# Gate and up projections as 2x2 block products with seven products for eight, and a down projection in four parts

## The chip, the cores and the metric

The kernel runs on one core of a Trainium2 chip. The metric is the device time of one execution in microseconds (us); lower is better. The engines are named as in the profile: PE is TensorE's matrix multiply and PEld its load of the stationary operand, DVE is VectorE, ACT is ScalarE, POOL is GpSimd, SP is SyncE, which here only issues transfers.

## The reference, cut to what matters

A decoder trunk of two layers works on 256 tokens of width 2048. A layer has a mixing part and then a SwiGLU feed-forward network (FFN), and the change lies in the latter:

```
h = rms_norm(x, norm_ffn_w)                            # (256, 2048)
x = x + (silu(h @ w_gate) * (h @ w_up)) @ w_down       # gate, up: 2048 x 5632; down: 5632 x 2048
```

All is float32.

## The kernel before, in words

**Split products.** A float32 number is split into a high half and a low half (a matmul type, fp32r, that PE takes at speed): `xh` and `xl` for activations, `wh` and `wl` for weights. Each product is three matmuls, high x high, low x high, high x low (L343, L344, L345), accumulated in PSUM. The activations are the stationary operand (128 tokens), and a weight tile of 512 columns moves through.

**Weight stream.** All weights of the program are one list of tiles (`plan`, L250), each of a pair of k-tiles: 128 partitions x 2 x 512 columns, 512 KB. `wtile` (L300) is called when PE needs the next tile. It issues loads ahead (`fetch`, L275, on SP's queue, into five `raw` buffers) and prepares the tile after the one in use (`split`, L284): ACT copies `raw` to `wh`, which rounds (L295), and DVE computes `wl = raw - wh` (L296). There are three buffers each of `wh` and `wl`. An engine carries out its instructions in program order; between engines they wait on semaphores for data and for buffers.

**FFN.** `ffn` (L204) goes through the 5632 hidden columns in 11 blocks of 512. For each block `dense` (L319) makes the gate: 8 tiles (pairs of k-tiles), each with 2 k-tiles x 2 token tiles x 3 matmuls. ACT applies silu out of PSUM, scaled by the row's reciprocal norm. A second `dense` makes up, and DVE multiplies the two (L216). The result is transposed by PE (L131) and split into halves `hh`, `hl`, which stay in two of the 22 general buffers (`U`) until the down projection. `FFN_PARTS = [8, 3]`: after 8 blocks, and again after 3, four groups of 512 output columns of the down projection are made from the blocks at hand and added to the residual in SBUF (`add_res`, L183). PSUM has four `dn` tiles for `dense` and four `mx` tiles for the rest.

**Output projection.** Ahead of the FFN, `out_proj` (L188) makes four groups of columns; after each, `post_x` (L354) transposes the new residual, scales it by the norm's weight and splits it into `xh` and `xl`, which the FFN uses.

GpSimd has next to no work in the FFN; it does some small operations of the mixing part (L104) there and in the norms.

Of the kernel before, what the change touches and what calls it, by code (L numbers as in the profile page):

```python
# [21 lines left out]
RWKV_EPS = 64e-5  # L22
EXP_HALF = math.exp(-0.5)

FFN_PARTS = [8, 3]

# [29 lines left out]
class Trunk:  # L56
# [121 lines left out]
    def setup(self):  # L178
        nc, A = self.nc, self.A
        self.plan()  # L180
        self.pp = [self.cp.tile([P, NPP], F32, tag=f"pp{l}", name=f"pp{l}") for l in range(DEPTH)]
# [66 lines left out]
    RAW, SPLIT = 5, 3  # L248

    def plan(self):  # L250
        seq = []
        for l in range(DEPTH):
            off = 0
            for n in (IN_W[name] for name in IN_ORDER):
                seq += [(f"win{l}", off + kp * 2 * P * n, n) for kp in range(8)]
                off += D * n
            for g in range(4):
                seq += [("wout", (l * 4 + g) * D * 512 + kp * 2 * P * 512, 512) for kp in range(8)]
            f0 = 0
            for nf in FFN_PARTS:  # L260
                for f in range(f0, f0 + nf):
                    for w in ("wgate", "wup"):
                        seq += [(w, (l * 11 + f) * D * 512 + kp * 2 * P * 512, 512) for kp in range(8)]
                for g in range(4):
                    seq += [("wdown", (l * 4 + g) * D_FF * 512 + kp * 2 * P * 512, 512)
                            for kp in range(2 * f0, 2 * (f0 + nf))]
                f0 += nf
        self.seq, self.loaded, self.cast, self.used = seq, [], [], 0

    @staticmethod  # L270
    def cuts(i, n):
# [11 lines left out]

    def split(self, upto):  # L284
        nc = self.nc
        while len(self.cast) < min(upto, len(self.seq)):
            i = len(self.cast)
            raw = self.loaded[i]
            if i < len(self.seq) - 2 * FFN_PARTS[-1]:
                wh = self.wp.tile([P, 1024], F32R, tag="wh", name=self.nm("wh"), bufs=self.SPLIT)  # L290
                wl = self.wp.tile([P, 1024], F32R, tag="wl", name=self.nm("wl"), bufs=self.SPLIT)
            else:
                wh, wl = self.U(F32R), self.U(F32R)
            for c in self.cuts(i, self.seq[i][2]):
                nc.scalar.activation(wh[:, c], raw[:, c], AF.Copy)  # L295
                nc.vector.tensor_tensor(wl[:, c], raw[:, c], wh[:, c].bitcast(F32), op=ALU.subtract)  # L296
            self.cast.append((wh, wl))
            self.loaded[i] = None

    def wtile(self, n):  # L300
        i = self.used
        assert self.seq[i][2] == n
        self.fetch(i + self.RAW)
        self.split(i + self.SPLIT - 1)
        self.fetch(i + self.RAW + self.SPLIT - 2)
        r = self.cast[i]
        self.cast[i] = None
        self.used += 1
        return r

# [8 lines left out]
    def dense(self, n, kps, xs, cm):  # L319
# [3 lines left out]
        ps = [self.dps(), self.dps()]  # L323
        last = len(kps) - 1
        for i, kp in enumerate(kps):
            wh, wl = self.wtile(n)
            for j in range(2):
                xh, xl = xs(2 * kp + j)
                st = i == 0 and j == 0
# [8 lines left out]
                else:  # L338
                    c = slice(j * n, (j + 1) * n)
                    for t in range(2):  # L340
# [3 lines left out]
                        nc.tensor.matmul(o, lhsT=xl[:, x], rhs=wh[:, c], start=False, stop=False)  # L344
                        nc.tensor.matmul(o, lhsT=xh[:, x], rhs=wl[:, c], start=False, stop=sp)  # L345
                self.pump()
        return ps


    def new_x(self):  # L350
        self.ssq = self.S(8)
        self.xt = []

    def post_x(self, l, g, wname):  # L354
# [3 lines left out]
        self.transpose_split(lambda t, k: self.res[g][:, t, k * P:(k + 1) * P], xh, xl,  # L358
                             lambda k: self.par(l, wname, g * 4 + k))
        self.xt.append((xh, xl))  # L360
        self.squares(g)

    def squares(self, g):
        sq = self.U()
# [823 lines left out]
    def out_proj(self, l):  # L1188
# [12 lines left out]
        self.finish_x()  # L1201
        self.yt = None

    def ffn(self, l):
        f0 = 0
        xt, rstd = self.xt, self.rstd
        for pi, nf in enumerate(FFN_PARTS):
            hts = []
            for f in range(f0, f0 + nf):
                kps = list(range(8))  # L1210
                ps = self.dense(512, kps, self.xs, False)
                sg = self.evac_tm(ps, 512, AF.Silu)
                ps = self.dense(512, kps, self.xs, False)
                for t in range(2):
                    o = sg[:, t * 512:(t + 1) * 512]
                    self.stt(o, ps[t], rstd[:, t:t + 1], o, ALU.mult, ALU.mult)
                hh = self.v4(self.U(F32R))
                hl = self.v4(self.U(F32R))
                self.transpose_split(lambda t, k: sg[:, t * 512 + k * P:t * 512 + (k + 1) * P], hh, hl, None)
                hts.append((hh, hl))  # L1220
            lastp = pi == len(FFN_PARTS) - 1

            def xs(k):
# [30 lines left out]
    def final(self, kps, xs, fw):  # L1254
# [8 lines left out]
        for t in range(2):  # L1263
            ps = self.dps()
            for i, kp in enumerate(kps):
                if t == 0:
                    ws.append(self.wtile(512))
                wh, wl = ws[i]
                for j in range(2):
                    xh, xl = xs(2 * kp + j)  # L1270
                    c, x = slice(j * 512, j * 512 + 512), slice(t * P, (t + 1) * P)
                    nc.tensor.matmul(ps, lhsT=xh[:, x], rhs=wh[:, c], start=i == 0 and j == 0, stop=False)  # L1272
                    nc.tensor.matmul(ps, lhsT=xl[:, x], rhs=wh[:, c], start=False, stop=False)  # L1273
                    nc.tensor.matmul(ps, lhsT=xh[:, x], rhs=wl[:, c], start=False, stop=i == len(kps) - 1 and j == 1)  # L1274
# [74 lines left out]
    return np.ascontiguousarray(w.reshape(k, 2, P, n).transpose(0, 2, 1, 3)).reshape(-1)  # L1349


def _layout(i):
    i = {k: np.asarray(v) for k, v in i.items()}
    o = {"cst": _constants(), "rm": _ret_mask()}
# [51 lines left out]
    wo, gate, up, down = [], [], [], []  # L1406
    for l in range(DEPTH):
        w = i["w_out"][l]
        part = {0: w[1536:], 1: w[512:1024], 2: w[1024:1536], 3: w[:512]}
        w = np.concatenate([part[n] for n in OUT_ORDER], axis=0)  # L1410
        wo += [_tiles(w[:, g * 512:(g + 1) * 512], 512) for g in range(4)]
        gate += [_tiles(i["ffn_w_gate"][l][:, g * 512:(g + 1) * 512], 512) for g in range(11)]
        up += [_tiles(i["ffn_w_up"][l][:, g * 512:(g + 1) * 512], 512) for g in range(11)]
        down += [_tiles(i["ffn_w_down"][l][:, g * 512:(g + 1) * 512], 512) for g in range(4)]
    o["wout"], o["wgate"], o["wup"], o["wdown"] = (np.concatenate(x) for x in (wo, gate, up, down))
    return o


# [20 lines left out]
```

## Time and profile before

| | |
|---|---|
| time, median of 3 runs (lowest, highest) | 2444.47 us (2444.41, 2446.57) |
| the profiled execution | 2444.33 us, of which the span from first to last instruction is 2442.3 us |
| granted TensorE clock, mean | 0.996 |
| HBM read | 430.66 MB, 178 GB/s over the span |

The profile is taken from one execution. Its page has: 1, the busy time of each engine; 2, the span in 40 slices; 3, the transfer queues; 4, the chain of work that ended last; 5, the costliest groups of instructions (line, engine, operation, output<-inputs, shape, count, busy us, mean ns, idle time ahead of them and what ended it); 6, the transfers. Further views list instructions in order of time (start in us, duration in us, engine, line, operation, and in brackets the idle time of the engine ahead of it with what ended it), and busy times by stretches of the span. `mx` and `dn` are PSUM tiles; `u`, `s`, `wh`, `wl`, `raw`, `xh`, `xl`, `res`, `cc`, `pp` and `vf` lie in SBUF. Matmuls overlap in the pipeline, so the distance of two starts, and not a duration, is what one costs.

### The profile page before, as it was taken

What the parts mean: (1) busy time and instruction counts of PE and PEld (TensorE: products, weight loads), DVE (VectorE), ACT (ScalarE), POOL (GpSimd) and SP (SyncE); (2) the same over time, 40 slices, a digit from 0 to 9 for tenths busy, and PEclk for the clock granted to TensorE, in tenths of its full rate; (3) what the DMA queues carried; (4) which work ended last, traced back from release to release, by engine and by line L of the source; (5) the groups of instructions that cost most, each with busy time, mean ns of one, the idle gap of its engine ahead of it and who ended that gap; (6) DMA issues with size and microseconds to landing.
All of it is one profiled execution on the core that took longest, in us unless ns stands there. A gap on an engine that the chain in (4) does not pass through costs nothing. (4 is left out here: it accounts for less than half of the span.)

```text
span 2442.3 us, 33197 instructions
## 1 busy us (share of the span) xinstructions
PE 2411.7 (99%) x13208; PEld 2050.3 (84%) x13208; DVE 1403.6 (57%) x1722; ACT 1113.1 (46%) x1376; POOL 138.4 (6%) x141
## 2 busy tenths in 40 slices
PE   8999999999999999999999999999999999999998
PEld 8998788888888888888899988888888888888886
DVE  7777656544544544445567876665445454444455
ACT  6445544444444433344454545444444444334444
POOL 3100230000000000000001022200000000000000
PEclk9999999999999999999999999999999999999999
DMA  8454445555555555655544544455555555556554
GB/s 292 147 168 113 146 159 164 186 186 190 188 190 191 188 190 189 207 191 188 181 147 156 166 116 141 156 173 180 190 192 187 191 190 188 190 190 207 192 186 147
DMA packets 139419, 435.97 MB, mean 179 GB/s; under 512 B 30464, under 2 KB 30720, under 8 KB 139264
## 3 DMA queue, kind: packets, MB, share of 16 engines
q1 hardware_dynamic: 137360, 428.52, 53.8%
q0 software_dynamic: 1184, 4.19, 0.5%
q8 instruction: 103, 1.69, 0.3%
q10 hardware_dynamic: 720, 1.15, 0.1%
q14 instruction: 52, 0.43, 0.0%
HBM read 430.66 MB, written 3.15 MB: 178 GB/s over the span
## 5 line engine op out<-in xcount | busy, mean ns | idle before, releaser
L296 DVE TENSOR_TENSOR wl<-raw,wh 128x1024 fp32r<-128x1024 f32 (+3 forms) x811 | 986.8, 1218 | 934.5 <-ACT wh L295 931.1
L295 ACT ACTIVATE wh<-raw 128x1024 fp32r<-128x1024 f32 (+3 forms) x811 | 844.7, 1042 | 1174.8 <-PE dn L344 998.2
L345 PE MATMUL dn<-wl,xh 128*128 128x512 f32 (+2 forms) x1856 | 713.9, 385 | 12.2 <-DVE wl L296 12.2
L343 PE MATMUL dn<-wh,xh 128*128 128x512 f32 (+2 forms) x1856 | 719.7, 388 | 0.0
L344 PE MATMUL dn<-wh,xl 128*128 128x512 f32 (+2 forms) x1856 | 714.2, 385 | 0.0
L345 PEld LDWEIGHTS dn<-wl,xh 128*128 128x128 f32 x1856 | 349.8, 189 | 78.6 <-DVE wl L296 13.6
L343 PEld LDWEIGHTS dn<-wh,xh 128*128 128x128 f32 x1856 | 349.9, 189 | 66.8 <-issue 1.4
L344 PEld LDWEIGHTS dn<-wh,xl 128*128 128x128 f32 x1856 | 349.9, 189 | 65.9 <-issue 1.4
L344 PE MATMUL dn<-wh,u 128*128 128x512 f32 x936 | 369.6, 395 | 0.0
L345 PE MATMUL dn<-wl,u 128*128 128x512 f32 x936 | 368.6, 394 | 0.0
L343 PE MATMUL dn<-wh,u 128*128 128x512 f32 x936 | 368.5, 394 | 0.0
L335 PE MATMUL dn<-xh,wh 128*128 128x256 f32 x896 | 258.5, 289 | 7.2 <-ACT wh L295 7.2
L337 PE MATMUL dn<-xh,wl 128*128 128x256 f32 x896 | 254.6, 286 | 1.1 <-DVE wl L296 1.1
L336 PE MATMUL dn<-xl,wh 128*128 128x256 f32 x896 | 254.9, 285 | 0.0
L343 PEld LDWEIGHTS dn<-wh,u 128*128 128x128 f32 x936 | 175.9, 188 | 39.8
L345 PEld LDWEIGHTS dn<-wl,u 128*128 128x128 f32 x936 | 176.3, 188 | 39.1
L344 PEld LDWEIGHTS dn<-wh,u 128*128 128x128 f32 x936 | 175.9, 188 | 39.6
L335 PEld LDWEIGHTS dn<-xh,wh 128*128 128x128 f32 x896 | 173.4, 194 | 10.0 <-ACT wh L295 7.7
L337 PEld LDWEIGHTS dn<-xh,wl 128*128 128x128 f32 x896 | 172.9, 194 | 1.8 <-DVE wl L296 1.5
L336 PEld LDWEIGHTS dn<-xl,wh 128*128 128x128 f32 x896 | 173.6, 194 | 0.3
L119 ACT ACTIVATE u<-mx 128x512 fp32r<-128x512 f32 (+4 forms) x158 | 73.5, 497 | 65.8 <-PE mx L127 30.2
L101 DVE TENSOR_TENSOR u<-u,u 128x1024 f32<-128x1024 f32 (+26 forms) x175 | 84.4, 487 | 22.5 <-POOL u L104 11.8
(142 smaller groups left out, 1157.6 us busy)
## 6 DMA issues: line engine op xcount, KB each, us to landing
raw<-wgate SPq DMA_DIRECT2D x176, 512.0 KB, 3.4
raw<-wup SPq DMA_DIRECT2D x176, 512.0 KB, 3.4
raw<-wdown SPq DMA_DIRECT2D x176, 512.0 KB, 3.5
raw<-win SPq DMA_DIRECT2D x175, 512.0 KB, 3.6
raw<-wout SPq DMA_DIRECT2D x64, 512.0 KB, 3.4
raw<-win SPq DMA_DIRECT2D x32, 340.0 KB, 2.9
raw<-win SPq DMA_DIRECT2D x16, 360.0 KB, 3.0
u<-xt SPq DMA_DIRECT2D x8, 256.0 KB, 7.7
```

The source lines that it names most:

```text
L101: self.nc.vector.tensor_tensor(out, a, b, op=op)
L119: self.nc.scalar.activation(out, in_, func, **kw)
L295: nc.scalar.activation(wh[:, c], raw[:, c], AF.Copy)
L296: nc.vector.tensor_tensor(wl[:, c], raw[:, c], wh[:, c].bitcast(F32), op=ALU.subtract)
L335: nc.tensor.matmul(o, lhsT=wh[:, c], rhs=xh, start=st and m % 2 == 0, stop=False)
L336: nc.tensor.matmul(o, lhsT=wh[:, c], rhs=xl, start=False, stop=False)
L337: nc.tensor.matmul(o, lhsT=wl[:, c], rhs=xh, start=False, stop=sp and m % 2 == 1)
L343: nc.tensor.matmul(o, lhsT=xh[:, x], rhs=wh[:, c], start=st, stop=False)
L344: nc.tensor.matmul(o, lhsT=xl[:, x], rhs=wh[:, c], start=False, stop=False)
L345: nc.tensor.matmul(o, lhsT=xh[:, x], rhs=wl[:, c], start=False, stop=sp)
```

## The change

The gate and up weights of a block are interleaved on the host: a load now brings one k-tile, with its 512 gate columns and its 512 up columns (`wgu`). For a pair of k-tiles, the two token tiles times two k-tiles of the activations are a 2x2 matrix of blocks A, and k-tiles times (gate, up) are a 2x2 matrix of blocks W. In pairs 1 to 6 (`SEVEN`) the product of the two is made in Winograd's form, from 7 block products in place of 8. In pairs 0 and 7 it is made plainly. All eight results accumulate over pairs: four PSUM tiles C for what goes straight to an output, four PSUM tiles M for what has to be combined.

- Weight side, in `split`: for a Strassen pair, three parts s0, s1, s2. For s0, GpSimd makes three sums of weight blocks into `u1` and `u2` (one operation of 1024 columns, with one operand repeated, and two of 512); the loaded blocks A11/A22 are split by ACT and DVE as before, and the half tile `b` with the remaining block as well. For s1 and s2, `u1` and `u2` are split by ACT and DVE. Parts of the plain pairs (kind "c") have their subtraction on GpSimd. All other tiles (kind "n") are split as before.
- Activation side, in `post_pair`: for each of pairs 1 to 6, four differences and sums of activation blocks (128 columns each) on GpSimd, then halves of them on ACT and DVE, once per layer.
- `gate_up` takes the place of two `dense` calls, and evacuates C and M with eight DVE operations on 512 columns that read PSUM, two that do not, and four on ACT. The transposes of the result are put off (`late`) until the next block's first pair, or the down projection's first tile, has been issued.
- `FFN_PARTS = [3, 3, 3, 2]`: the down projection is made in four parts.

```
-FFN_PARTS = [8, 3]
+FFN_PARTS = [3, 3, 3, 2]
+SEVEN = range(1, 7)
...
+            elif kind == "c":
+                self.cast.append(halve(raw, [slice(0, 1024)], nc.gpsimd))
+            elif kind == "s0":
+                r1 = self.loaded[i + 1]
+                u1, u2 = self.U(), self.U()
...
+                nc.gpsimd.tensor_tensor(v(u1), v(raw), h(r1, 1).rearrange("p (o c) -> p o c", o=1).to_broadcast([P, 2, 512]),
+                                        op=ALU.add)
+                nc.gpsimd.tensor_tensor(h(u2, 0), h(u1, 0), h(raw, 1), op=ALU.add)
+                nc.gpsimd.tensor_tensor(h(u2, 1), h(u2, 0), h(r1, 0), op=ALU.add)
+                wh, wl = halve(raw, [slice(0, 1024)])
+                b = self.U(F32R)
+                nc.scalar.activation(h(b, 0), h(r1, 0), AF.Copy)
+                nc.vector.tensor_tensor(h(b, 1), h(r1, 0), h(b, 0).bitcast(F32), op=ALU.subtract)
+                self.cast.append((wh, wl, b))
+                self.sums = (u1, u2)
...
+                self.cast.append(halve(self.sums[int(kind[1]) - 1][:, :1024], [slice(0, 1024)]))
...
+    def gate_up(self, rstd):
...
+                *w, b21 = self.wtile(("s0",))
+                prod(M[0], A(0, 0), blk(w, 0), first, last)
+                prod(C[1], Q, blk(w, 1), False, False)
+                prod(C[0], A(0, 1), (b21[:, 0:512], b21[:, 512:1024]), False, False)
+                w = self.wtile(("s1",))
+                prod(M[1], S1, blk(w, 0), first, last)
+                prod(M[2], S3, blk(w, 1), first, last)
+                w = self.wtile(("s2",))
+                prod(M[3], S2, blk(w, 0), first, last)
+                prod(C[2], A(1, 1), blk(w, 1), False, False)
...
+        self.tt(c0, v, C[0], ALU.add)
+        self.act(c0, c0, AF.Silu, scale=rstd[:, 0:1])
+        self.tt(w_, w_, C[1], ALU.add)
+        self.stt(c0, w_, rstd[:, 0:1], c0, ALU.mult, ALU.mult)
+        self.tt(v, M[1], y, ALU.subtract)
+        self.tt(c1, y, C[2], ALU.add)
+        self.act(c1, c1, AF.Silu, scale=rstd[:, 1:2])
+        self.tt(v, v, C[3], ALU.add)
+        self.stt(c1, v, rstd[:, 1:2], c1, ALU.mult, ALU.mult)
```

Here `halve` casts to `wh` on ACT and subtracts to `wl` on DVE, or on the engine that is named, and `prod` issues the three matmuls of a block product.

More of the change, by code (lines that the diff above doesn't have):

```diff
@@ L180, in setup @@
         self.plan()
+        self.late = []
         self.pp = [self.cp.tile([P, NPP], F32, tag=f"pp{l}", name=f"pp{l}") for l in range(DEPTH)]
@@ L250, in plan, with plain @@
     def plan(self):
-        seq = []
+        seq, parts, done = [], [], []
+        def plain(tiles, kind="n"):
+            for t in tiles:
+                parts.append((kind, len(seq)))
+                seq.append(t)
+                done.append(len(seq))
         for l in range(DEPTH):
@@ L254, in plan @@
             for n in (IN_W[name] for name in IN_ORDER):
-                seq += [(f"win{l}", off + kp * 2 * P * n, n) for kp in range(8)]
+                plain((f"win{l}", off + kp * 2 * P * n, n) for kp in range(8))
                 off += D * n
             for g in range(4):
-                seq += [("wout", (l * 4 + g) * D * 512 + kp * 2 * P * 512, 512) for kp in range(8)]
+                plain(("wout", (l * 4 + g) * D * 512 + kp * 2 * P * 512, 512) for kp in range(8))
             f0 = 0
@@ L261, in plan @@
                 for f in range(f0, f0 + nf):
-                    for w in ("wgate", "wup"):
-                        seq += [(w, (l * 11 + f) * D * 512 + kp * 2 * P * 512, 512) for kp in range(8)]
+                    for kp in range(8):
+                        t = [("wgu", ((l * 11 + f) * 16 + 2 * kp + j) * P * 1024, 512) for j in range(2)]
+                        if kp in SEVEN:
+                            parts += [(f"s{j}", len(seq)) for j in range(3)]
+                            seq += t
+                            done += [len(seq)] * 3
+                        else:
+                            plain(t, "c")
                 for g in range(4):
-                    seq += [("wdown", (l * 4 + g) * D_FF * 512 + kp * 2 * P * 512, 512)
-                            for kp in range(2 * f0, 2 * (f0 + nf))]
+                    plain(("wdown", (l * 4 + g) * D_FF * 512 + kp * 2 * P * 512, 512)
+                          for kp in range(2 * f0, 2 * (f0 + nf)))
                 f0 += nf
-        self.seq, self.loaded, self.cast, self.used = seq, [], [], 0
+        self.seq, self.parts, self.done = seq, parts, done
+        self.loaded, self.cast, self.used = [], [], 0
     @staticmethod
@@ L285, in split @@
         nc = self.nc
-        while len(self.cast) < min(upto, len(self.seq)):
-            i = len(self.cast)
-            raw = self.loaded[i]
-            if i < len(self.seq) - 2 * FFN_PARTS[-1]:
-                wh = self.wp.tile([P, 1024], F32R, tag="wh", name=self.nm("wh"), bufs=self.SPLIT)
-                wl = self.wp.tile([P, 1024], F32R, tag="wl", name=self.nm("wl"), bufs=self.SPLIT)
-            else:
[L293 to L297, printed above, removed]
-            self.loaded[i] = None
@@ L300, in wtile, with halve @@
[L300 to L307, printed above, removed]
+        def halve(raw, cuts, eng=nc.vector):
+            wh = self.wp.tile([P, 1024], F32R, tag="wh", name=self.nm("wh"), bufs=self.SPLIT)
+            wl = self.wp.tile([P, 1024], F32R, tag="wl", name=self.nm("wl"), bufs=self.SPLIT)
+            for c in cuts:
+                nc.scalar.activation(wh[:, c], raw[:, c], AF.Copy)
+                eng.tensor_tensor(wl[:, c], raw[:, c], wh[:, c].bitcast(F32), op=ALU.subtract)
+            return wh, wl
@@ new lines, in split @@
+        while len(self.cast) < min(upto, len(self.parts)):
+            p = len(self.cast)
+            kind, i = self.parts[p]
+            raw = self.loaded[i]
+            if kind == "n" and i >= len(self.seq) - 2 * FFN_PARTS[-1]:
+                wh, wl = self.U(F32R), self.U(F32R)
+                nc.scalar.activation(wh[:, :1024], raw, AF.Copy)
+                nc.vector.tensor_tensor(wl[:, :1024], raw, wh[:, :1024].bitcast(F32), op=ALU.subtract)
+                self.cast.append((wh, wl))
+            elif kind == "n":
+                self.cast.append(halve(raw, self.cuts(i, self.seq[i][2])))
+            elif kind == "c":
[3 more added lines that the diff above has]
+                u1, u2 = self.U(), self.U()
+                h = lambda t, j: t[:, j * 512:(j + 1) * 512]
+                v = lambda t: t[:, :1024].rearrange("p (a c) -> p a c", a=2)
+                nc.gpsimd.tensor_tensor(v(u1), v(raw), h(r1, 1).rearrange("p (o c) -> p o c", o=1).to_broadcast([P, 2, 512]),
[8 more added lines that the diff above has]
+                self.sums = (u1, u2)
+                self.loaded[i + 1] = None
+            else:
+                self.cast.append(halve(self.sums[int(kind[1]) - 1][:, :1024], [slice(0, 1024)]))
+            self.loaded[i] = None
@@ L308, in wtile @@
+    def wtile(self, kinds=("n",)):
+        p = self.used
+        assert self.parts[p][0] in kinds, (self.parts[p], kinds)
+        upto = min(p + self.SPLIT - 1, len(self.parts))
+        self.fetch(self.done[upto - 1])
+        if len(self.cast):
+            self.fetch(self.done[len(self.cast) - 1] + self.RAW)
+        self.split(upto)
+        self.fetch(self.done[upto - 1] + self.RAW)
+        r = self.cast[p]
+        self.cast[p] = None
         self.used += 1
@@ L346, in dense, with flush @@
                 self.pump()
+            self.flush()
         return ps
+    def flush(self):
+        for f in self.late:
+            f()
+        self.late = []
     def new_x(self):
@@ L352, in new_x @@
         self.xt = []
+        self.comb = {}
     def post_x(self, l, g, wname):
@@ L357, in post_x, with post_pair @@
         xl = self.xp.tile([P, 4, 256], F32R, tag="xl", name=self.nm("xl"))
-        self.transpose_split(lambda t, k: self.res[g][:, t, k * P:(k + 1) * P], xh, xl,
-                             lambda k: self.par(l, wname, g * 4 + k))
+        src = lambda t, k: self.res[g][:, t, k * P:(k + 1) * P]
+        scale = lambda k: self.par(l, wname, g * 4 + k)
+        if wname == "nfw":
+            for b in range(2):
+                self.post_pair(2 * g + b, lambda t, k: src(t, 2 * b + k), lambda k: scale(2 * b + k),
+                               xh[:, 2 * b:2 * b + 2, :], xl[:, 2 * b:2 * b + 2, :])
+        else:
+            self.transpose_split(src, xh, xl, scale)
         self.xt.append((xh, xl))
         self.squares(g)
+    def post_pair(self, kp, src, scale, xh, xl):
+        fl = lambda t: t.rearrange("p a b -> p (a b)")
+        ps = self.PS()
+        for k in range(2):
+            for t in range(2):
+                self.tr(ps[:, k * 256 + t * P:k * 256 + (t + 1) * P], src(t, k), self.ident)
+        w = self.U()
+        for k in range(2):
+            self.act(w[:, k * 256:(k + 1) * 256], ps[:, k * 256:(k + 1) * 256], AF.Copy, scale=scale(k))
+        self.act(fl(xh), w[:, :512], AF.Copy)
+        self.tt(fl(xl), w[:, :512], fl(xh).bitcast(F32), ALU.subtract)
+        if kp in SEVEN:
+            a11, a21, a12, a22, s1, s2, s3, q = [w[:, i * P:(i + 1) * P] for i in range(8)]
+            self.tt(s1, a21, a22, ALU.subtract, eng="pool")
+            self.tt(s2, s1, a11, ALU.subtract, eng="pool")
+            self.tt(s3, a11, a21, ALU.subtract, eng="pool")
+            self.tt(q, a12, s2, ALU.add, eng="pool")
+            c = self.U(F32R)
+            self.act(c[:, 0:512], w[:, 512:1024], AF.Copy)
+            self.tt(c[:, 512:1024], w[:, 512:1024], c[:, 0:512].bitcast(F32), ALU.subtract)
+            self.comb[kp] = c
     def squares(self, g):
@@ L1202, in out_proj, with prod, finish @@
         self.yt = None
+    def gate_up(self, rstd):
+        mm = self.nc.tensor.matmul
+        def prod(o, x, w, start, stop):
+            for i, (a, b) in enumerate(((0, 0), (1, 0), (0, 1))):
+                mm(o, lhsT=x[a], rhs=w[b], start=start and i == 0, stop=stop and i == 2)
+        C = [self.dps() for _ in range(4)]
+        M = None
+        blk = lambda w, j: tuple(t[:, j * 512:(j + 1) * 512] for t in w)
+        for kp in range(8):
+            xk = [self.xs(2 * kp + j) for j in range(2)]
+            A = lambda t, k: tuple(h[:, t * P:(t + 1) * P] for h in xk[k])
+            if kp not in SEVEN:
+                for k in range(2):
+                    w = self.wtile(("c",))
+                    for t in range(2):
+                        for n in range(2):
+                            prod(C[2 * t + n], A(t, k), blk(w, n), kp == 0 and k == 0, kp == 7 and k == 1)
+            else:
+                cb = self.comb[kp]
+                S1, S2, S3, Q = [(cb[:, i * P:(i + 1) * P], cb[:, 512 + i * P:512 + (i + 1) * P]) for i in range(4)]
+                first, last = kp == SEVEN[0], kp == SEVEN[-1]
+                if first:
+                    M = [self.PS() for _ in range(4)]
+                *w, b21 = self.wtile(("s0",))
[8 more added lines that the diff above has]
+                prod(C[2], A(1, 1), blk(w, 1), False, False)
+            if kp == 0:
+                self.flush()
+            if kp == SEVEN[-1]:
+                t0, t1, sg = self.U(), self.U(), self.U()
+                z, w_, y, v = t0[:, 0:512], t0[:, 512:1024], t1[:, 0:512], t1[:, 512:1024]
+                c0, c1 = sg[:, 0:512], sg[:, 512:1024]
+                self.act(v, M[0], AF.Copy)
+                self.tt(z, v, M[3], ALU.add)
+                self.tt(w_, M[1], z, ALU.subtract)
+                self.tt(y, M[2], z, ALU.add)
+        hh, hl = self.v4(self.U(F32R)), self.v4(self.U(F32R))
+        self.tt(c0, v, C[0], ALU.add)
[7 more added lines that the diff above has]
+        self.stt(c1, v, rstd[:, 1:2], c1, ALU.mult, ALU.mult)
+        def finish(t):
+            ps = self.PS()
+            for k in range(4):
+                self.tr(ps[:, k * P:(k + 1) * P], sg[:, t * 512 + k * P:t * 512 + (k + 1) * P], self.ident)
+            o, p4 = hh[:, :, t * P:(t + 1) * P], ps.rearrange("p (k c) -> p k c", k=4)
+            self.act(o, p4, AF.Copy)
+            self.tt(hl[:, :, t * P:(t + 1) * P], p4, o.bitcast(F32), ALU.subtract)
+        self.late += [lambda: finish(0), lambda: finish(1)]
+        return hh, hl
@@ L1207, in ffn @@
         for pi, nf in enumerate(FFN_PARTS):
[L1208 to L1220, printed above, removed]
+            hts = [self.gate_up(rstd) for f in range(f0, f0 + nf)]
             lastp = pi == len(FFN_PARTS) - 1
@@ L1349, in _tiles, with _pairs @@
     return np.ascontiguousarray(w.reshape(k, 2, P, n).transpose(0, 2, 1, 3)).reshape(-1)
+def _pairs(a, b):
+    k = a.shape[0] // (2 * P)
+    w = np.stack([a.reshape(k, 2, P, 512), b.reshape(k, 2, P, 512)], axis=2).transpose(0, 1, 3, 2, 4)
+    o = np.empty((k, 2, P, 2, 512), w.dtype)
+    for kp in range(k):
+        if kp in SEVEN:
+            o[kp, 0, :, 0], o[kp, 0, :, 1], o[kp, 1, :, 0], o[kp, 1, :, 1] = \
+                w[kp, 0, :, 0], w[kp, 1, :, 1], w[kp, 1, :, 0], w[kp, 0, :, 1]
+        else:
+            o[kp] = w[kp]
+    return o.reshape(-1)
 def _layout(i):
@@ L1405, in _layout @@
     o["rw2"], o["ra2"], o["rg2"] = np.stack(w2s), np.stack(a2s), np.ascontiguousarray(np.stack(g2s))
-    wo, gate, up, down = [], [], [], []
+    wo, gu, down = [], [], []
     for l in range(DEPTH):
@@ L1411, in _layout @@
         wo += [_tiles(w[:, g * 512:(g + 1) * 512], 512) for g in range(4)]
-        gate += [_tiles(i["ffn_w_gate"][l][:, g * 512:(g + 1) * 512], 512) for g in range(11)]
-        up += [_tiles(i["ffn_w_up"][l][:, g * 512:(g + 1) * 512], 512) for g in range(11)]
+        gu += [_pairs(i["ffn_w_gate"][l][:, g * 512:(g + 1) * 512], i["ffn_w_up"][l][:, g * 512:(g + 1) * 512])
+               for g in range(11)]
         down += [_tiles(i["ffn_w_down"][l][:, g * 512:(g + 1) * 512], 512) for g in range(4)]
-    o["wout"], o["wgate"], o["wup"], o["wdown"] = (np.concatenate(x) for x in (wo, gate, up, down))
+    o["wout"], o["wgu"], o["wdown"] = (np.concatenate(x) for x in (wo, gu, down))
     return o
```

5 lines of the change are left out of this document (3 added, 2 removed).

## The prediction, made before the change had run

> **What bounds the kernel now.** I read the page's busy times first, then the chain that ended last, then stretches of the timeline.
>
> ```profile
> span 2442.3 us, 33197 instructions
> PE 2411.7 (99%) x13208; PEld 2050.3 (84%) x13208; DVE 1403.6 (57%) x1722; ACT 1113.1 (46%) x1376; POOL 138.4 (6%) x141
> ```
>
> ```profile
> 1745.68 0.66 PE mx L131 x6
> 1790.14 0.66 PE mx L131 x6
> ```
>
> ```profile
> 599.66 0.39 PE L345 MATMUL dn<-wl,xh 128*128 128x512 f32 x1
> ...
> 605.10 0.39 PE L345 MATMUL dn<-wl,xh 128*128 128x512 f32 x1
> ```
>
> TensorE (PE) is busy all the time and GpSimd (POOL) hardly works. The two rows of the chain are the transposes that close two consecutive FFN blocks of 512 columns: 44.46 us for one block of gate and up. The two timeline rows lie 24 matmuls apart: 5.44 us, so 0.2267 us for one matmul of 512 columns. A block has 192 of them (2 matrices x 8 k-tile pairs x 2 k-tiles x 2 token tiles x 3 split terms): 43.5 us, and 0.9 us for its transposes and hand-overs. So gate and up run at the rate of PE; weight load, casts and transfers lie beside it.
>
> **The saving on PE.** In six of the eight pairs the 8 block products become 7, each of 3 matmuls: 6 x 3 = 18 matmuls fewer, 174 left. 18 x 0.2267 = 4.08 us for a block, which would then take 44.46 - 4.08 = 40.4 us. There are 22 blocks (11 in each of 2 layers): 89.8 us. If nothing else were late, the profiled execution of 2444.3 us (span 2442.3 and 2.0 around it; the median of the runs is 2444.5, so I use them as one) would become 2354.5.
>
> **What is added for it.** In a block each Strassen pair now makes three weight tiles of 1024 columns and a half tile (b), each with a cast on ACT and a subtraction on VectorE (DVE), and three sums on POOL: one of 1024 and two of 512. The four tiles of the two plain pairs get their subtraction on POOL. Prices, without contention:
>
> ```profile
> L296 DVE TENSOR_TENSOR wl<-raw,wh 128x1024 fp32r<-128x1024 f32 x761 | 936.6, 1232 | 914.3 <-ACT wh L295 911.2
> L101 DVE TENSOR_TENSOR res<-res,dn 128x512 f32<-128x512 f32 x48 | 33.0, 688 | 10.8 <-PE dn L345 5.6 <-PE dn L1274 4.9
> L296 DVE TENSOR_TENSOR wl<-raw,wh 128x512 fp32r<-128x512 f32 x2 | 1.4, 692 | 1.3 <-ACT wh L295 1.3
> ```
>
> ```profile
> L295 ACT ACTIVATE wh<-raw 128x1024 fp32r<-128x1024 f32 x179 | 189.8, 1061 | 272.4 <-PE dn L344 272.3
> L119 ACT ACTIVATE u<-mx 128x512 fp32r<-128x512 f32 x16 | 8.7, 597 | 5.1 <-PE mx L131 5.1
> ```
>
> ```profile
> 1352.06 2.41 POOL L104 TENSOR_TENSOR u<-vf,u 128x1024 f32<-128x1024 f32 x1 [6.43 <-DVE u L115]
> ```
>
> ```profile
> 1558.61 1.30 POOL L104 TENSOR_TENSOR u<-u,u 128x512 f32<-128x512 f32 x1 [5.12 <-DVE u L101]
> ```
>
> ```profile
> L104 POOL TENSOR_TENSOR u<-cc,ah x8: 1894/1898/2877, 258.1 to 1524.4; 128x1024 fp32r<-128x1024 f32 x8
> L104 POOL TENSOR_TENSOR u<-u,cc x16: 722/1178/1721, 307.2 to 1552.8; 128x256 f32<-128x256 f32 x16
> ```
>
> ACT: 22 casts x 1.06, six of 512 and five evacuations of about 0.6: 30 us for a block. DVE: 18 x 1.23 + 6 x 0.69, and some twelve operations of 512 that empty PSUM at 0.69: 35 us. Both stay under 40.4.
>
> POOL: two full inputs cost 2.41 us for 1024 and 1.30 for 512. The first sum of a pair repeats one 512-column operand. Two rows price a repeat: 1.89 us for 1024 where single values are repeated inside (L104, cc and ah), and 0.72 as the least for 256 where a whole stretch is repeated (u and cc). 0.72, 1.30 and 2.41 lie on one line, so a repeated stretch saves nothing; that is the form of the new sum, and I take 2.41 (1.89 would be 3.1 us less for a block). A pair: 2.41 + 2 x 1.30 = 5.01. A block: 6 x 5.01 + 4 x 2.41 = 39.7 us, beside 40.4 of PE. Taken one by one, all engines fit, POOL only just.
>
> **They do not run side by side.** This decides the forecast. Where POOL reads SBUF, a DVE operation with both inputs in SBUF stands still:
>
> ```profile
> 1352.88 2.67 DVE L296 TENSOR_TENSOR wl<-raw,wh 128x1024 fp32r<-128x1024 f32 x1 [0.99 <-ACT wh L295]
> ```
>
> ```profile
> 265.51 1.90 POOL L104 TENSOR_TENSOR u<-cc,ah 128x1024 fp32r<-128x1024 f32 x1
> 267.36 2.52 POOL L104 TENSOR_TENSOR u<-cc,s 128x1024 fp32r<-128x1024 f32 x1
> ```
>
> ```profile
> 265.52 2.60 DVE L296 TENSOR_TENSOR wl<-raw,wh 128x680 fp32r<-128x680 f32 x1
> ```
>
> ```profile
> 1460.99 2.52 POOL L104 TENSOR_TENSOR u<-cc,ah 128x1024 fp32r<-128x1024 f32 x1
> ```
>
> ```profile
> 1461.78 0.42 DVE L101 TENSOR_TENSOR s<-mx,s 128x256 f32<-128x256 f32 x1
> ```
>
> The first subtraction started at 1352.88 beside the POOL operation that ran until 1354.47 and ended 1.08 us after that: 1.59 of waiting and 1.08 of work. The second was shut out from 265.52 to 267.41 and ended at 268.12. POOL's next one then waited for DVE in its turn: it was issued at 267.36, and ended 1.76 us after DVE did, 0.14 less than the 1.90 it takes alone. So they alternate, and what overlaps is only the start of the one that waits. The last two rows are the counter-example: with one input in PSUM (mx), DVE took 0.42 us in the middle of a POOL operation. So the evacuations are free of this, and the weight subtractions are not.
>
> Time of a block in which either has the shared path:
> - a Strassen pair: POOL 5.01, less 3 x 0.14 for overlapped starts, is 4.59; DVE 3 x 1.08 and 0.55 for the half tile (0.69 less the same 0.14) is 3.79. Together 8.38, where PE needs 21 x 0.2267 = 4.76.
> - six pairs 50.3; four POOL subtractions 9.64; two multiplications of the two SBUF halves (the last step of each token tile) 1.1. Together 61.0 us, against 40.4 of PE.
>
> The path becomes the bound. It will not be busy without a break: the cast on ACT (1.06) stands between a sum and its subtraction, only three wh and wl buffers exist, and a raw pair is released only after DVE has read it, with five raw buffers and this landing time:
>
> ```profile
> raw<-wgate SPq DMA_DIRECT2D x176, 512.0 KB, 3.4
> ```
>
> With POOL one pair ahead, two pairs of raw tiles are held and one buffer is left, so a new pair's second tile is asked for when DVE has done a subtraction and a half tile with POOL's first two sums between them (2.3 + 1.1 + 1.2 + 0.6 = 5.2 us into a cycle) and lands 3.4 later, at 8.6; that alone makes a pair 8.4 to 8.9 us. I take 3% on the 61.0: 63 us for a block, 18.5 more than now. 22 x 18.5 = 407, so 2444.3 + 407 = 2851 us.
>
> The bounds. If each start is wholly hidden (POOL's three rows have a slope of 2.2 ns a column, so 4.5 a pair; DVE 3.7), a block has 49 + 9 + 1 = 59 us: 2764. If nothing overlaps, a pair is 5.01 + 3 x 1.23 + 0.69 = 9.39 and a block 56.3 + 9.6 + 1.4 = 67.3: 2947.
>
> The Trainium skill, page "SBUF — State Buffer", section "Who interferes with whom", calls the shared pair an exclusive lock that a GpSimd operation, or a VectorE operation with two SBUF inputs, has for its whole instruction while the other fully blocks. Taken by the letter that is the 2947 above; the trace agrees on the block, but its 1.08 after the release, against 1.23 alone, shows the start overlapped, so I keep the smaller sum.
>
> **The other edits.** The new waits stand in POOL's queue: the plain tiles' subtractions come behind the sums of the pair in front, and PE waits for them as for all wl tiles; this is in the sum. On SP each raw load waits for a buffer that POOL also reads; counted above. The four products' PSUM tiles of a block must be emptied before the next block starts; the first three are complete 0.68 to 2.04 us (3 to 9 matmuls) before the last, so PE would lose under a microsecond, and it waits for weights anyway: 0, at most 22 x 0.7 = 15 us. The down projection in four parts has the same matmuls; its 32 more adds into the residual (0.69 each, 22 us in all, one input in PSUM) lie beside 2.72 us of PE per tile, of which DVE uses 1.23: 0. The input combinations are 48 POOL operations of 128 columns, under 0.72 us each, in the output projection, where POOL is idle; the last are needed about seven k-tile pairs later: 0, at most 6 us.
>
> **The rivals.**
>
> *PE stays the bound (faster).* If POOL and DVE overlapped after all, 39.7 and 35 us would hide under 40.4: 2354.5 us. For it speaks each engine's own sum; against it every contended row above, and that the path's 61.0 would have to shrink by 27% to get below today's 44.46, the point from which it decides. Chance 0.06.
>
> *POOL cannot run ahead.* The sums come from the 22 shared buffers, of which six hold combinations, up to six finished blocks, three an open evacuation. If a pair's sums have to wait until DVE has read the pair before, the order is serial: POOL 5.0, with the first subtraction and the half tile in between (1.6), then cast 1.06 and subtraction 1.23, and the same again overlapped only in part: about 9.4 for a pair, 67 for a block, 2940 us. Chance 0.15.
>
> *The clock falls too.* PE now pauses. Two rows of the view by stretches (length, then busy us and count of PE, weight load, DVE, ACT, POOL, then granted clock, DMA share, GB/s), and PE's timeline in the first of them:
>
> ```profile
> 260.00:270.00 10.00, 3.98 (x17) 3.22 (x16) 10.00 (x7) 1.97 (x3) 9.88 (x5) 0.71 0.08 19
> ```
>
> ```profile
> 310.00:320.00 10.00, 8.81 (x46) 7.21 (x45) 4.96 (x6) 2.82 (x3) 5.72 (x5) 1.00 0.20 62
> ```
>
> ```profile
> 261.22 0.32 PE L343 MATMUL dn<-wh,xh 128*128 128x340 f32 x1
> ...
> 261.84 0.31 PE L344 MATMUL dn<-wh,xl 128*128 128x340 f32 x1
> 268.18 0.65 PE L345 MATMUL dn<-wl,xh 128*128 128x340 f32 x1 [6.03 <-DVE wl L296]
> 268.63 0.49 PE L343 MATMUL dn<-wh,xh 128*128 128x340 f32 x1
> ...
> 270.61 0.48 PE L344 MATMUL dn<-wh,xl 128*128 128x340 f32 x1
> ```
>
> This is the change in small: POOL and DVE fully busy, PE waiting 6.03 us for wl, and afterwards one matmul per 0.283 us (7 in 1.98) where it was 0.155 (4 in 0.62). A pause of 1.2 us (310 to 320) left the clock at 1.00. In the new blocks about 3.6 us of pause spread over three tiles of a pair, so single pauses are nearer to the 1.2. If the clock falls nevertheless, a matmul of 512 costs 0.2267 x 0.283/0.155 = 0.414: 174 of them are 72 us, over the path's 61, and the block becomes 73: 2444 + 22 x 28.5 = 3071 us. Chance 0.12. The Trainium skill, page "TensorE: Matmul & The Clock Gate", section "Why this matters for your kernels", asks for no idle gaps over about 3 us between bursts; no gap of that length is in this trace, only 1.2 and 6.03.
>
> **How the numbers follow.** Forecast, the shared path as the bound, 0.67: 2851. Serial sums 0.15, clock 0.12, PE-bound 0.06. The range goes from below the hidden-start bound (2764, less 20 for the extras) to above the serial case, part of the way to the clock case: 2745 to 3010; outside are the faster case, about two thirds of the clock case and the forecast's tails, under 0.2. A difference of 0.2% (5 us) is about what a measurement of this kernel can tell; all but the PE-bound case are far above it: faster 0.06, same 0.01, slower 0.93.
>
> **What would show it.** The page after should have PE at 80 to 85% of a span of about 2850, POOL at 870 us or more with its own waits inside, and much of DVE's time in weight subtractions (wl) that last about 2 us or more in place of 1.23; PE's idle time should be put down to DVE wl and POOL wl. Blocks should be some 63 us apart, the stages outside gate and up unchanged, the granted clock near 1. I am wrong if subtractions still last 1.23 us beside POOL sums, if PE shows no waits, or if the time lost lies in the down projection.

## The result, and the profile after

The changed kernel takes 2845.5 us (median of 4 runs, 2840.32 to 2847.25) against 2445.3 us before (2444.41 to 2446.57): a ratio of 1.163, 95% interval 1.161 to 1.165. It is 400 us slower; 2851 had been forecast. The profiled execution took 2845.22 us.

The head of the page after, then the slices of GpSimd's busy time, and of the granted clock:

```profile
span 2843.4 us, 34300 instructions
PE 2504.0 (88%) x12812; PEld 2033.5 (72%) x12812; DVE 2202.6 (77%) x2102; ACT 1344.6 (47%) x1690; POOL 1304.7 (46%) x673
...
POOL 2103213883587088548201032048826771883581
PEclk9999999899999999998999999998899889899989
```

PE has 396 matmuls fewer, and yet the span is longer; DVE has 800 us more, POOL 1166. POOL's digits are the FFN stages: 7 or 8 while gate and up are made, near 0 in the down projection. Two pieces of the chain that ended last, the plain pairs of two consecutive blocks:

```profile
1959.04 4.14 PE dn L1294 x18
2022.01 4.11 PE dn L1294 x18
```

The blocks are 63.0 us apart, where they were 44.46. Over the whole kernel 400.2 us on 22 blocks make 44.46 + 18.2 = 62.7. Groups by line and shape (count, busy us, mean ns, idle before and its releaser), and then PE's waits (in total, times, longest):

```profile
L308 DVE TENSOR_TENSOR wl<-raw,wh 128x1024 fp32r<-128x1024 f32 x543 | 772.1, 1425 | 354.2 <-ACT wh L307 352.7
L308 DVE TENSOR_TENSOR wl<-u,wh 128x1024 fp32r<-128x1024 f32 x264 | 575.3, 2200 | 24.5 <-ACT wh L307 24.2
L336 DVE TENSOR_TENSOR u<-raw,u 128x512 fp32r<-128x512 f32 x132 | 244.4, 1852 | 25.3 <-ACT u L335 25.2
L103 DVE TENSOR_TENSOR u<-u,dn 128x512 f32<-128x512 f32 x88 | 58.1, 682 | 28.4 <-PE dn L1294 28.2
```

```profile
PE mx L1294 <- DVE wl L308: 231.6, 149, 3.4
PE mx L1294 <- DVE u L103: 32.4, 14, 2.3
PE dn L1294 <- POOL wl L308: 20.0, 10, 3.6
PE dn L1294 <- DVE u L103: 16.1, 13, 1.3
```

The subtractions of the two sum tiles last 2.20 us in place of 1.23, the half tile (L336) 1.85 in place of 0.69. The evacuation that reads PSUM (`u<-u,dn`) lasts 0.68, as before. PE waits mostly for wl tiles of DVE. How the engines take turns, on POOL's timeline and on DVE's, in the middle of a block:

```profile
577.87 2.16 POOL L331 TENSOR_TENSOR u<-u,raw 128x512 f32<-128x512 f32 x1
580.11 2.13 POOL L332 TENSOR_TENSOR u<-u,raw 128x512 f32<-128x512 f32 x1
582.20 2.88 POOL L329 TENSOR_TENSOR u<-raw,raw 128x1024 f32<-128x1024 f32 x1
...
589.49 3.39 POOL L329 TENSOR_TENSOR u<-raw,raw 128x1024 f32<-128x1024 f32 x1
```

```profile
578.80 2.31 DVE L308 TENSOR_TENSOR wl<-raw,wh 128x1024 fp32r<-128x1024 f32 x1
581.03 1.76 DVE L336 TENSOR_TENSOR u<-raw,u 128x512 fp32r<-128x512 f32 x1
```

POOL ends at 580.03; DVE, waiting since 578.80, ends 1.08 us later at 581.11. POOL's next sum, waiting since 580.11, ends at 582.24, 1.13 after that. DVE's half tile ends at 582.79, 0.55 after. POOL's next, 1024 columns, ends at 585.08, 2.29 after. One turn each, with nothing side by side but the start of the one that waits.

### The profile page after: what moved, and what is told of

It reads as the page before. It is cut to its first block, busy times and chain, and to the rows that moved or that the text cites. A ratio compares the mean times of both kernels' runs of the same rounds, so it can differ in the third digit from the quotient of the medians.

```text
span 2843.4 us, 34300 instructions
## 1 busy us (share of the span) xinstructions
PE 2504.0 (88%) x12812; PEld 2033.5 (72%) x12812; DVE 2202.6 (77%) x2102; ACT 1344.6 (47%) x1690; POOL 1304.7 (46%) x673
## 5 line engine op out<-in xcount | busy, mean ns | idle before, releaser
L307 ACT ACTIVATE wh<-raw 128x1024 fp32r<-128x1024 f32 (+2 forms) x681 | 705.4, 1038 | 744.0 <-PE dn L391 429.2
L308 DVE TENSOR_TENSOR wl<-u,wh 128x1024 fp32r<-128x1024 f32 x264 | 575.3, 2200 | 24.5 <-ACT wh L307 24.2
L329 POOL TENSOR_TENSOR u<-raw,raw 128x1024 f32<-128x1024 f32 x132 | 390.7, 2960 | 396.0 <-DMA raw<-wgu 265.5
L307 ACT ACTIVATE wh<-u 128x1024 fp32r<-128x1024 f32 x264 | 278.5, 1058 | 450.1 <-PE mx L1294 229.8
L308 POOL TENSOR_TENSOR wl<-raw,wh 128x1024 fp32r<-128x1024 f32 x88 | 220.2, 2518 | 246.0 <-ACT wh L307 246.0
L1294 PE MATMUL mx<-wh,u 128*128 128x512 f32 x792 | 277.8, 435 | 32.4 <-DVE u L103 32.4
L332 POOL TENSOR_TENSOR u<-u,raw 128x512 f32<-128x512 f32 x132 | 268.9, 2037 | 9.3
L336 DVE TENSOR_TENSOR u<-raw,u 128x512 fp32r<-128x512 f32 x132 | 244.4, 1852 | 25.3 <-ACT u L335 25.2
L331 POOL TENSOR_TENSOR u<-u,raw 128x512 f32<-128x512 f32 x132 | 259.0, 1962 | 7.5
L1294 PE MATMUL dn<-wl,xh 128*128 128x512 f32 x484 | 202.9, 419 | 20.0 <-POOL wl L308 20.0
L1294 PE MATMUL dn<-wh,xh 128*128 128x512 f32 x484 | 203.2, 420 | 16.1 <-DVE u L103 16.1
```

The costliest lines, as they stand in the source:

```text
L308: eng.tensor_tensor(wl[:, c], raw[:, c], wh[:, c].bitcast(F32), op=ALU.subtract)
L329: nc.gpsimd.tensor_tensor(v(u1), v(raw), h(r1, 1).rearrange("p (o c) -> p o c", o=1).to_broadcast([P, 2, 512]), op=ALU.add)
L331: nc.gpsimd.tensor_tensor(h(u2, 0), h(u1, 0), h(raw, 1), op=ALU.add)
L332: nc.gpsimd.tensor_tensor(h(u2, 1), h(u2, 0), h(r1, 0), op=ALU.add)
L336: nc.vector.tensor_tensor(h(b, 1), h(r1, 0), h(b, 0).bitcast(F32), op=ALU.subtract)
L1294: mm(o, lhsT=x[a], rhs=w[b], start=start and i == 0, stop=stop and i == 2)
```

## The experiments

**The down projection alone.** The kernel before with the new list of parts:

```
-FFN_PARTS = [8, 3]
+FFN_PARTS = [3, 3, 3, 2]
```

> The kernel before with the down projection in four parts alone. The prediction priced this at nothing, because the 32 more adds into the residual lie beside matmuls: 2445 us, within 5 us of the kernel before. If the adds or the more frequent changes between gate/up and down were on the path, the 32 adds of 0.69 us would show: up to 2467 us.

Measured: 2445.28 us against 2445.47; ratio 0.9996 (0.9986 to 1.0006). Four parts cost nothing. The 400 us belong to gate and up and to what was added for them.

**The sums without their reading.** In the changed kernel fills take the place of the sums, so this kernel leaves out part of the computation:

```
-nc.gpsimd.tensor_tensor(v(u1), v(raw), ..., op=ALU.add)
-nc.gpsimd.tensor_tensor(h(u2, 0), h(u1, 0), h(raw, 1), op=ALU.add)
-nc.gpsimd.tensor_tensor(h(u2, 1), h(u2, 0), h(r1, 0), op=ALU.add)
+for n in (1024, 1024, 512):
+    nc.gpsimd.memset(u1[:, :n], 0.5)
+for j in range(2):
+    for n in (512, 512, 256):
+        nc.gpsimd.memset(u2[:, j * 512:j * 512 + n], 0.5)
```

> The changed kernel, with the three weight sums of each pair on GpSimd replaced by fills with a constant that keep GpSimd busy for about as long (near 5 us a pair) but read nothing; the sums themselves are left out. Shared path: the VectorE subtractions fall from about 2 us to 1.23 us, a block comes down to 41 to 45 us, and the kernel takes 2360 to 2460 us. GpSimd just too slow, or unable to run ahead (the serial rival): its occupation is the same, so blocks stay at 60 us or more and the time above 2780 us. If anything else of the seven-product scheme (ACT, more tiles per pair, PSUM) held it up, the time also stays above 2600 us.

Measured: 2391.6 us, ratio 0.978 (0.977 to 0.980), a block 42.0 us. The page's second line, then groups of DVE and of POOL:

```profile
PE 2344.1 (98%) x12812; PEld 1970.9 (83%) x12812; DVE 1686.3 (71%) x2102; ACT 1338.8 (56%) x1690; POOL 1004.9 (42%) x1465
```

```profile
L308 DVE TENSOR_TENSOR wl<-u,wh 128x1024 fp32r<-128x1024 f32 x264 | 319.2, 1223 | 89.8 <-ACT wh L307 87.7
L337 DVE TENSOR_TENSOR u<-raw,u 128x512 fp32r<-128x512 f32 x132 | 100.1, 759 | 24.2 <-ACT u L336 24.2
```

```profile
L333 POOL MEMSET u<- 128x512 f32 x528 | 275.2, 542 | 1.2
L330 POOL MEMSET u<- 128x1024 f32 x264 | 255.9, 969 | 0.0
```

POOL is still busy for 1005 us, with nine fills of 0.33 to 0.97 us for a pair, but DVE's subtractions are back at 1.223 us. So it is not that POOL is busy, nor the number of tiles, casts or PSUM banks; it is POOL's reading while DVE reads two operands from SBUF. The fills also do without the raw tiles, so the run takes away POOL's waits for those as well. That the reading is the cause rests on the length of DVE's subtractions (2.20 us against 1.22) and on the turns shown above. (The Trainium skill, page "SBUF — State Buffer", section "Who interferes with whom", makes the same distinction: a VectorE instruction with two SBUF inputs contends with a GpSimd instruction that reads SBUF, not with one that only writes. This run agrees.) Some 54 of the 89.8 us that the seven products can save on PE by the prediction arrive here; what takes the rest stays open.

**The plain tiles back on VectorE.**

```
-                self.cast.append(halve(raw, [slice(0, 1024)], nc.gpsimd))
+                self.cast.append(halve(raw, [slice(0, 1024)]))
```

> The changed kernel with the subtractions of the four plain tiles of a block back on VectorE; the sums stay on GpSimd. Sum over the shared path for a block: 6 x 8.38 + 4 x 1.08 + 1.1 = 55.7 us in place of 61.0, so if the path is the bound throughout, about 57.5 us a block and 2730 us. If the end of a block is set by the order of the work (GpSimd has finished its sums ahead and VectorE, ACT and PE catch up in turn, GpSimd waiting 10 us for the next cast), GpSimd's plain tiles are not what is late, and the time stays within 30 us of 2845.

Measured: 2810.1 us, 35 us below the changed kernel, ratio to before 1.149 (1.147 to 1.151). That is nearer to the second expectation, just outside its 30 us, than to the first: 5.2 us less of the path in a block gave 1.6. A block within a part shows why. First POOL's timeline of the changed kernel; then the stretch of PE's plain pairs and that of its six seven-product pairs, in the changed kernel and in this run (length, busy us and count of PE, weight load, DVE, ACT, POOL, then clock, DMA share, GB/s):

```profile
800.30 7.13 POOL L308 TENSOR_TENSOR wl<-raw,wh 128x1024 fp32r<-128x1024 f32 x3 [11.00 <-ACT wh L307]
807.40 2.44 POOL L329 TENSOR_TENSOR u<-raw,raw 128x1024 f32<-128x1024 f32 x1
809.80 2.83 POOL L308 TENSOR_TENSOR wl<-raw,wh 128x1024 fp32r<-128x1024 f32 x1
...
850.65 2.15 POOL L332 TENSOR_TENSOR u<-u,raw 128x512 f32<-128x512 f32 x1
863.27 7.15 POOL L308 TENSOR_TENSOR wl<-raw,wh 128x1024 fp32r<-128x1024 f32 x3 [10.47 <-ACT wh L307]
```

```profile
801.89:815.10 13.21, 11.93 (x52) 9.37 (x51) 10.90 (x11) 6.44 (x8) 13.13 (x7) 1.00 0.47 153
815.10:864.87 49.77, 36.89 (x133) 27.34 (x132) 46.56 (x26) 22.58 (x26) 38.67 (x17) 0.86 0.40 128
```

```profile
792.31:807.83 15.52, 12.41 (x52) 9.29 (x51) 15.32 (x14) 6.43 (x8) 11.22 (x6) 1.00 0.36 120
807.83:854.46 46.63, 35.34 (x133) 25.10 (x131) 44.96 (x27) 22.59 (x26) 28.27 (x13) 0.93 0.40 141
```

In the changed kernel POOL makes the sums of six pairs from 807.40 to 852.80, with the fourth plain subtraction among them, and ends two pairs ahead of PE. Then nothing is ready for it for 10.5 us, until ACT's cast of the next plain tile, which waits for PE. In those 10.5 us DVE makes its remaining subtractions at full speed. While the plain tiles are used, POOL is busy for 13.13 of 13.21 us, and DVE's evacuations, which read PSUM, lie beside POOL's subtractions. In the experiment DVE makes the plain subtractions and the evacuations one after the other: it is busy for 15.32 of 15.52 us there, and for 60.3 of 62.2 us in the block. The six pairs became 3.1 us shorter, the plain tiles 2.3 longer. So my first expectation left out DVE's own queue. The 55.7 us of the path and ten evacuations from PSUM behind one another (0.60 us each, as the next run shows) come to 61.7 us; this is an estimate, against a mean of 61.0 measured. The reading comes from the timelines and was not tested by a run of its own.

**Everything on VectorE.** The same line, and the three sums with `nc.vector` for `nc.gpsimd`.

> The changed kernel with all weight sums and the plain subtractions on VectorE; GpSimd does nothing for gate and up. If the two engines really take turns on one path, GpSimd's help costs more than it saves: a pair's sums hold the path 4.6 us from GpSimd, and VectorE makes them itself in 1.22 + 2 x 0.69 = 2.6 us. VectorE then needs 6 x 6.98 + 4 x 1.23 + 8.4 = 55 us a block, and the kernel takes 2680 to 2750 us, 100 us or more below the changed kernel. If GpSimd's sums were largely hidden beside VectorE and something else set the 63 us (three buffers, ACT in between), another 16 us of work for VectorE makes it no faster: 2845 us or above.

Measured: 2552.3 us, ratio to before 1.044 (1.042 to 1.045), and 293 us less than the changed kernel. A block takes 49.3 us, less than the 55 that I had worked out. DVE's timeline:

```profile
578.37 1.22 DVE L329 TENSOR_TENSOR u<-raw,raw 128x1024 f32<-128x1024 f32 x1
579.50 1.22 DVE L308 TENSOR_TENSOR wl<-raw,wh 128x1024 fp32r<-128x1024 f32 x1
580.64 0.69 DVE L331 TENSOR_TENSOR u<-u,raw 128x512 f32<-128x512 f32 x1
581.24 1.22 DVE L308 TENSOR_TENSOR wl<-u,wh 128x1024 fp32r<-128x1024 f32 x1
```

An operation of 1.22 us is followed by the next after 1.13 or 1.14, one of 0.69 after 0.60: back to back, durations overlap, and the distance is the cost. By distances a pair costs DVE 4 x 1.135 + 3 x 0.60 = 6.35 us and a block 6 x 6.35 + 4 x 1.135 + 12 x 0.60 = 49.8; measured are 49.3. DVE alone does in 6.35 us what DVE and POOL together did in over 8. (The Trainium skill, page "GPSIMD Engine Reference", section "4.1 Engine selection", sends element-wise work on two inputs to VectorE for speed; this case agrees, with 1.22 us against 2.41 for 1024 columns, and here it would hold even if GpSimd's time were free, because that time is taken from VectorE.)

**Fewer pairs with seven products.** With 3 pairs, PE needs 42.4 us for a block. Sums on GpSimd, plain tiles on VectorE:

```
-SEVEN = range(1, 7)
+SEVEN = [1, 3, 5]
```

> The changed kernel with seven products in pairs 1, 3 and 5 only, plain products in the other five, and the plain subtractions on VectorE. PE needs 43.5 - 3 x 0.68 + 0.9 = 42.4 us for a block, the shared path 3 x 8.38 + 10 x 1.08 + 1.1 = 37.1 us. If the sum over the path is what counts and the three buffers bridge a pair of 8.4 us and the plain one next to it (together 10.5 us of path beside 10.2 of PE), a block takes 42.5 to 44.5 us: 2400 to 2445 us, no slower than before. If every seven-product pair stalls PE on its own, by 3.6 us, a block takes 53 us: 2640 us.

Measured: 2513.4 us, ratio 1.028 (1.026 to 1.029), between the two expectations: 47.5 us a block. PE waits for DVE 66 times, mostly in the plain pair behind a seven-product pair (the `dn` row below). POOL's first sum was mostly put down to a late raw tile, which led to the next run, with `RAW, SPLIT = 8, 3` and 19 general buffers.

> Seven products in pairs 1, 3 and 5 with the sums on GpSimd and the plain subtractions on VectorE (2513 us with five raw buffers), now with eight raw buffers, paid for with three of the 22 general ones. In that run GpSimd's first sum waited for its raw tile each time, up to 8 us, and PE then 1.8 to 2.4 us for the part made from it. If the late raw tiles are the cause, the sums start earlier and the time comes down to 2400 to 2460 us. If the shared path itself delays the subtractions, it stays above 2490 us.

Measured: 2523.7 us, ratio 1.032 (1.030 to 1.033). More raw tiles, with three general buffers fewer, did not help. POOL's wait for its raw tiles fell (866 to 242 us in total), and others took its place; whether the general buffers given up are the cause was not tested, and why the sums still start late stays open. Then the three sums on VectorE as well:

> As with everything on VectorE, but seven products only in pairs 1, 3 and 5. VectorE: 3 x 6.98 + 10 x 1.23 + 8.4 = 41.7 us a block, PE 42.4. If VectorE's own time is all that counts, a block takes 43 to 45.5 us: 2410 to 2465 us. If each seven-product pair stalls PE because its tiles are made too late (as with the sums on GpSimd: 2513 us), 2490 us or more.

Measured: 2408.2 us, ratio 0.985 (0.984 to 0.986): 1.5% below the kernel before, with the interval clear of 1, and a block of 42.8 us. PE's waits for DVE in gate and up, first with the sums on GpSimd, then on VectorE:

```profile
PE dn L1294 <- DVE wl L308: 35.6, 51, 2.0
PE mx L1294 <- DVE wl L308: 27.3, 15, 3.0
```

```profile
PE mx L1294 <- DVE wl L308: 0.9, 1, 0.9
```

The two kernels differ only in the engine that makes three sums in three pairs of a block: 105 us. Of these, 62 are the waits shown. PE's own 13010 matmuls were busy for another 35 us (2410.9 against 2375.8), at a granted clock of 0.991 against 0.997. With two pairs, `SEVEN = [2, 5]`, and with four, `[1, 3, 4, 6]`:

> All sums and subtractions on VectorE, seven products in pairs 2 and 5 only. Counted by the distance of back-to-back starts (1.135 us for 1024 columns, 0.60 for 512, from the run with all six pairs on VectorE), VectorE needs 2 x 6.35 + 12 x 1.135 + 12 x 0.60 = 33.5 us a block, PE 43.1. PE-bound: 2445 - 22 x 2 x 0.68 = 2415 us, some 7 us above the run with three pairs (2408). If spreading costs a fixed amount that the three-pair run hides, it is level with that run or better.

Measured: 2427.1 us, ratio 0.993 (0.992 to 0.995). Saved are 17 us of the 30 that PE gains; with three pairs it was 37 of 45. Why the rest does not arrive stays open.

> The same with pairs 1, 3, 4 and 6. VectorE needs 4 x 6.35 + 8 x 1.135 + 7.2 = 41.7 us a block, and PE 44.46 - 4 x 0.68 = 41.7: level. If the three buffers even out the two, 2390 to 2405 us, a little below the run with three pairs. If the order inside a block decides (a pair needs 6.35 us of VectorE beside 4.76 of PE, and the block's evacuation 7.2 in one piece), VectorE's lag is not made up and it takes 2410 to 2450 us.

Measured: 2408.5 us, ratio 0.985 (0.984 to 0.987), level with three pairs. PE's further 15 us do not arrive. By the sum DVE is then as long as PE, but that this is the cause is not shown: PE's waits for DVE in gate and up come to only 4 us. Three pairs with the sums on VectorE is the version to keep.

**A filled PE.** Three matmuls with a zero operand ahead of each part of a pair, in the changed kernel:

```
+                def fill(w):
+                    for i in range(3):
+                        mm(C[i], lhsT=self.zero, rhs=w[0][:, 0:512], start=False, stop=False)
...
+                fill(w)
```

> The changed kernel with three more matmuls ahead of each of the three parts of a pair, whose stationary operand is zero, so that they add nothing; 54 x 0.2267 = 12.2 us more PE work a block, to shorten its pauses and keep the clock up. If the shared path is the bound, PE has 22 us to spare in a block: the granted clock rises from 0.95 towards 1.0 and the time stays within 25 us of 2845. If the fallen clock costs time in the changed kernel, the time falls by 30 us or more. If PE's own work were on the path, it rises by up to 270 us.

Measured: 2979.3 us, 134 us above the changed kernel; ratio to before 1.219 (1.217 to 1.220). The granted clock rose from 0.95 to 0.976. So half of the added PE work, 6.1 of 12.2 us a block in the mean, lengthens the kernel, which I had not expected. POOL's waits at the turn of a block grew, from 10.5 us to

```profile
615.25 2.41 POOL L310 TENSOR_TENSOR wl<-raw,wh 128x1024 fp32r<-128x1024 f32 x1 [14.39 <-ACT wh L309]
```

The path explains it. By the timelines of POOL and DVE it is held for 61.6 us of the block from 825.14 to 892.10, as in the changed kernel, but stands free for 5.3 us in place of 1.6, in the catching up at the end. There PE is late and not the path, for each cast waits for PE to free its buffer. This block grew by 4.0 us; the first block behind a down projection grew by 11 (759.43 to 825.14, against 747.18 to 801.89), and why it grew more stays open. What the fallen clock itself costs cannot be read from this run, as it adds work and clock at once.

## Why the prediction was right, and what its sum could not tell

*The saving on PE.* Of the 4.08 us a block, 2.5 arrive in the run without reads (a block of 42.0 us), and with three pairs on VectorE 1.7 of 2.04 (42.8 us). What takes the rest stays open.

*Prices alone.* 2.41 us for a full sum of 1024 on POOL was right (2.44 at 807.40, with one operand repeated, while DVE read PSUM), and so was 1.30 for 512 by the sums' distances from DVE's ends (1.13 plus the overlapped start).

*They do not run side by side.* Shown by the turns, 1.08, 1.13, 0.55 and 2.29 us against 1.08, 1.16, 0.55 and 2.27 in the sum, and by the run without reads. In a pair these come to 8.38 us as forecast.

*The time of a block: right as a sum, not in its order.* The path is held while POOL reads SBUF or DVE works on two SBUF operands. In the block from 801.89 to 864.87 (62.98 us) the two timelines leave only 1.6 us in which neither does, so it is held for 61.4 us, where the sum had 61.0 and 3% beside it. Five more blocks give 61.1 to 61.7 us, with 1.3 to 2.9 free. So the mechanism and the size of the sum hold. The six pairs are not six equal pairs of 8.38, though. POOL has three operations in a pair and DVE four, and they alternate one for one; so POOL gets to its next pair after 7.3 us (582.20 to 589.49), and a part of DVE's share is left over for the end, after POOL has stopped at 852.80.

*What the sum could not tell.* It says how long the path is held, and not what each of its terms is worth. With the plain tiles on VectorE the sum gave 115 us less, and 35 came: DVE's evacuations had been lying beside POOL's plain subtractions, and in the experiment DVE's own queue (60.3 us) was longer than the path. The prediction set the evacuations aside as free of the path, which is right, but they take DVE's time.

*The 3%.* It was not worked out, so its size is luck. The free time stands where ACT's casts are late at the end of a block (0.26, 0.91, 0.18 and 0.25 us ahead of DVE and POOL). The 8.4 to 8.9 us that I gave a pair because of the raw tiles did not show: POOL runs ahead at 7.3 us a pair.

*The other edits.* The down projection's parts cost nothing, as forecast, and were measured alone. For the emptying of the PSUM tiles at most 15 us of waiting were allowed; PE waited 48.5 us for it (`DVE u L103`, 32.4 and 16.1). POOL's plain subtractions made PE wait 20.0 us, nine times of ten in the first plain pair behind a down projection.

*The rivals.* That GpSimd and VectorE overlap: excluded. That POOL cannot run ahead: it was two pairs ahead (its sums for the last two pairs were done at 852.80, while PE used the first plain tile of the next block some 13 us later). That the clock falls: it did in part, to 0.86 in the stretch of the six pairs above and to 0.95 in the mean, where I had expected it near 1 (and PE busy for 80 to 85%; it was 88%). PE's single pauses in that stretch were as long as 3.05 us, and not near 1.2. My list of pauses in the kernel before, only 1.2 and 6.03, had also missed one of 4.42 us, at 1487.84. In the block above the path was free for 1.6 us, so a faster PE alone could have given back no more than that, some 35 us over 22 blocks by estimate.

## What to carry to other kernels

An idle engine is not free help: before work is moved to GpSimd, look in the trace for one GpSimd operation that reads SBUF beside a VectorE operation with two SBUF operands, and measure from the end of the one to the end of the other. Where they take turns, add the two engines' times, and compare with what the busier engine needs to do both jobs itself; here it was 6.35 us against more than 8. A sum that fits tells how long the path is held, and not what one of its terms is worth: try an edit that takes away a single term, and first sum up the whole queue of the engine that gets the work, with what it does off the path.

## What the runs showed of the hardware

- While both have work that needs the path, the two engines alternate one operation for one, however long each is (the turns of 1.08, 1.13, 0.55 and 2.29 us). A queue of VectorE operations on two SBUF operands is held to the pace of GpSimd's next ones (a pair in 7.3 us), and catches up only when GpSimd stops (10.5 us at the end of a block).
- Back-to-back VectorE operations of 1024 columns lie 1.135 us apart though each lasts 1.22.
- The clock fell after shorter pauses than I had taken from the kernel before (where 1.2 us did nothing). PE's timeline of the changed kernel:

```profile
595.71 0.50 PE L1294 MATMUL mx<-wl,u 128*128 128x512 f32 x1 [2.71 <-DVE wl L308]
...
598.53 0.63 PE L1294 MATMUL dn<-wh,xh 128*128 128x512 f32 x1
598.96 0.63 PE L1294 MATMUL dn<-wh,xl 128*128 128x512 f32 x1
599.38 0.57 PE L1294 MATMUL dn<-wl,xh 128*128 128x512 f32 x1
599.79 0.40 PE L1294 MATMUL mx<-wh,xh 128*128 128x512 f32 x1
600.03 0.40 PE L1294 MATMUL mx<-wh,xl 128*128 128x512 f32 x1
```

Behind pauses of up to 2.71 us the matmuls lie 0.43 us apart, and 0.23 again from 599.79 on, some 4 us after PE had resumed.
